# Mix to next product in a two-layer decoder trunk: tile 0 ends three weight tiles early, its first transposes move into the mix, the next product goes two chunks ahead

## Chip, cores and metric

The kernel runs on one core of a Trainium2 chip, as one launch. The metric is device time in microseconds, the median of several runs. Engines are named as in the profile: PE (TensorE matmul), PEld (its weight loads), DVE (VectorE), ACT (ScalarE), POOL (GpSimd), SP (the queue that issues the loads).

## The reference, cut to what matters

256 tokens of width 2048 pass two layers. Layer 0 mixes with a Mamba-2 block, layer 1 with sliding-window attention on one shared K/V; each layer has a SwiGLU network of width 5632. Around every sub-layer stands an RMS norm before and one after:

```
h = h + rmsnorm(mix, g[1])
ffn = (silu(u @ w_gate) * (u @ w_up)) @ w_down      # u = rmsnorm(h, g[2])
h = h + rmsnorm(ffn, g[3])
k, v = split(rmsnorm(h, kv_norm_w) @ w_kv)           # once, between the layers
```

So at four places a product ("mix") of 256 x 2048 is normed, added to h, normed again and multiplied by the next weights. Three of them have a product behind them, and those are where the change lies.

## The kernel before

Everything is float32. A float32 operand is split into a high part in the matmul's own format and a low rest, and a product is three matmuls: high by high, high by low, low by high (lines 293 to 295). Weights are streamed by `Weights`: raw tiles of 512 KB in five buffers, filled by SP; ACT casts the high part (`whi`, line 77), DVE subtracts the low part (`wlo`, line 78), into **four** converted buffers each. One converted tile ("weight tile" from here on) holds 2 x 128 rows of the contraction by 512 columns; with one token tile it makes 6 matmuls, with both 12. For K/V and q the cast carries a scale, in two halves or four quarters (lines 73 and 74). A converted buffer is free once its last matmul has read it.

The 256 tokens are two tiles t = 0, 1 of 128. `mix_stage` makes the mix in four column chunks c of 512, each chunk and tile in a PSUM bank; there are eight banks, and the mix fills them all. For the last chunk the weight tiles at the end (`lag` of them) are held: tile 0 takes all of them first, then tile 1, so that tile 0 is done while tile 1 still works. When a tile is done, ACT squares the chunk (line 351), DVE makes the mean (`ms`, line 187), POOL the power -0.5 (`rs`, line 189), and DVE multiplies the chunk by the gain (line 354).

`a_first` is the product behind a mix. For a chunk c and a tile t its `step` adds the mix to h on DVE (`add_residual`, line 398: one bank to one chunk of h), transposes that chunk of h by four PE matmuls with the identity (line 205) into a bank, and splits the four pieces into high (ACT, line 214) and low (DVE, line 215) in `xx`; for K/V, which has no gain here, the whole chunk is split at once (lines 181 and 182). `prod` then makes the matmuls of chunk c and tile t. Since the row factor is only applied to the result, the product can start before the whole row is known: `row_factor` squares the new h on ACT (line 197, eight of 128 x 512) and yields the factor (`ms` on DVE, `rs` on POOL). The gate product's result passes through Silu with that factor as scale. After K/V, `to_row` puts the two factors on a diagonal (`dg`, DVE) and multiplies it by ones on PE (line 450), for q.

Each engine runs its own queue in order. The order is made when the program is built, by a scheduler with priorities: `tc.high_priority()` moves work ahead, `tc.keep_in_program_order` holds an instruction at its written place.

Of the kernel before, what the change touches and what calls it, by code (L numbers as in the profile page):

```python
# [10 lines left out]
AF = mybir.ActivationFunctionType  # L11
# [3 lines left out]
P = 128  # L15
T = 256
NT = 2
# [80 lines left out]
def tile_yoco(ctx: ExitStack, tc: tile.TileContext, a: dict):  # L98
# [92 lines left out]

    def norm_stats(pool, h, t):
        ss = pool.tile([P, 4], F32, tag="ss", name="ss", bufs=4)
        for c in range(4):
            hs = h[:, t, CW * c : CW * (c + 1)]
            junk = pool.tile([P, CW], mybir.dt.bfloat16, tag="junk", name="junk", bufs=2)
            nc.scalar.activation(junk[:], hs, AF.Square, accum_out=ss[:, c : c + 1])  # L197
        return rstd_of(pool, ss[:], D)

    def to_xt(src, t, c, g, xt):  # L200

        xh, xl, _ = xt
        pt = bank()
        for k in range(4):
            nc.tensor.transpose(pt[:, P * k : P * (k + 1)], src[:, P * k : P * (k + 1)], ident[:])  # L205
        if g is None:
            split_bank(xh[:, 4 * c : 4 * c + 4, P * t : P * (t + 1)], xl[:, 4 * c : 4 * c + 4, P * t : P * (t + 1)],
                       pt[:].rearrange("p (k t) -> p k t", k=4))
            return
        for k in range(4):  # L210
            kt = 4 * c + k
            ps = pt[:, P * k : P * (k + 1)]
            dh = xh[:, kt, P * t : P * (t + 1)]
            nc.scalar.activation(dh, ps, AF.Copy, scale=g[:, kt : kt + 1])  # L214
            nc.vector.scalar_tensor_tensor(xl[:, kt, P * t : P * (t + 1)], ps, g[:, kt : kt + 1],  # L215
                                           dh.bitcast(F32), ALU.mult, ALU.subtract)
# [123 lines left out]

    def mix_stage(key, xt, kts, layer, which, bk0=None, hook=None, lag=2):

# [14 lines left out]
        for c in range(4):  # L357
# [15 lines left out]
            else:  # L373
# [25 lines left out]

    def a_first(key, mix, g, xt):  # L400

        xh, xl = xt[:2]
        done = [0, 0]

        def update(c, t):
            while done[t] < min(c + 1, 4):
                add_residual(mix, t, done[t])
                done[t] += 1  # L410

        def step(c, t):
            with tc.high_priority():
                update(c, t)
                to_xt(h[:, t, CW * c : CW * (c + 1)], t, c, g, xt)
                update(c + 1, t)

        bk = []

        def prod(c, t, subs):  # L420
            if len(bk) == t:
                bk.append(bank())
            for n, (hi, lo, _, per) in enumerate(subs):
                for kk in range(per):
                    a_mm(bk, xh, xl, hi, lo, kk, 4 * c + SUB * n + kk, KD, 0, CW, ts=(t,))
# [12 lines left out]
        return bk  # L438

    def row_factor():  # L440

        return [norm_stats(hpool, h, t) for t in range(NT)]

# [15 lines left out]

    def ffn(layer, mix):  # L460
        xt = new_xt()
        with tc.tile_pool(name="ffn%d" % layer, bufs=1, side="right") as fp:
# [22 lines left out]
            for u in range(FF // CW):  # L485
                if u == 0:
                    gb = a_first("gate%d_%d" % (layer, u), mix, gt[:, layer, 2, :], xt)
# [13 lines left out]
    mix = mix_stage("wout", (yh, yl), DI // P, 0, 1, bk0=bk0)  # L501
    ypool.__exit__(None, None, None)
    mix = ffn(0, mix)


    with tc.tile_pool(name="attn", bufs=1, side="right") as ap:
        xt = new_xt()
        kvb = a_first("kv", mix, None, xt)
# [3 lines left out]
        mix = mix_stage("wo", ot, KD, 1, 1, hook=hook)  # L512


    mix = ffn(1, mix)
    for t in range(NT):
# [451 lines left out]
```

## Time and profile before

| what | value |
|---|---|
| median of 3 runs | 2436.85 us (2436.16 to 2437.26) |
| the profiled execution | 2436.95 us, span 2435.2 us |
| PE busy | 2405.5 us (99%), 11760 matmuls |
| DVE busy | 1450.1 us (60%) |
| ACT busy | 1222.4 us (50%) |
| DMA | 453.75 MB, mean 186 GB/s |
| chain that ended last | PE 95%, DVE 2%, ACT 2%, DMA 1% |

The span is the profiled execution from its first to its last instruction; the rest of the time lies around it. A matmul's row gives the line, the engine, `out<-in` by the program's names, and in brackets the idle time before it with what ended it. Matmuls overlap, so the start of one to the start of the next is their pace, not their duration.

### The profile page before, as it was taken

Reading aid. Unit: us, or ns where it says so; the run is one execution under the profiler, and the core shown is the slowest. Engines: PE = TensorE matmul, PEld = TensorE weight load, DVE = VectorE, ACT = ScalarE, POOL = GpSimd, SP = SyncE. Lnnn points to the kernel's source line nnn. Section 1 sums busy time; section 2 is a strip of 40 time slices with the busy share of each in tenths; the row PEclk is TensorE's granted clock in tenths of the full one; section 3 lists DMA queues with packets and bytes.
Section 4 is the critical chain, followed back from the end, with each engine's and each line's share of the span. In section 5 each row is a group of like instructions: output and inputs, shape, how many; then the busy total and the mean of one; then the engine's idle time right before and its main releaser. Section 6 shows DMA issues by size and latency. Waiting matters only on the chain.

```text
span 2435.2 us, 30881 instructions
## 1 busy us (share of the span) xinstructions
PE 2405.5 (99%) x11760; PEld 1995.0 (82%) x11760; DVE 1450.1 (60%) x2016; ACT 1222.4 (50%) x1733; POOL 82.7 (3%) x66
## 2 busy tenths in 40 slices
PE   7999999999999999999999999999999999999998
PEld 6888888888878888888888878777888888888887
DVE  6788888875464545445444468865545445454444
ACT  6576766664454444444444457755544444444443
POOL 1500000000000000000000000000000000000000
PEclk9999999999999999999999999999999999999999
DMA  6666666657656666666666664445666666666664
GB/s 202 175 205 193 191 189 191 187 175 244 192 166 196 188 189 193 185 191 191 204 194 193 194 192 152 130 126 160 199 190 190 185 194 186 191 191 206 194 194 145
DMA packets 283892, 453.75 MB, mean 186 GB/s; under 512 B 16976, under 2 KB 115536, under 8 KB 282976
## 3 DMA queue, kind: packets, MB, share of 16 engines
q1 hardware_dynamic: 283568, 451.45, 61.8%
q8 instruction: 92, 1.51, 0.3%
q14 instruction: 56, 0.46, 0.1%
q10 hardware_dynamic: 144, 0.26, 0.0%
q0 software_dynamic: 32, 0.07, 0.0%
HBM read 449.56 MB, written 2.16 MB: 185 GB/s over the span
## 4 chain that ended last, share of the span: by engine, by line
PE 95%; DVE 2%; ACT 2%; DMA 1%; issue 1%; POOL 0%; SPq 0%; DVEq 0%; POOLq 0%; ACTq 0%
PE bank L294 23%; PE bank L295 23%; PE bank L293 23%; PE bank L235 13%; PE bank L240 7%; PE bank L479 1%; DVE wlo L78 1%; PE bank L846 1%; PE bank L889 1%; PE bank L684 1%; ACT xx L214 0%; PE bank L881 0%; ACT junk L197 0%; PE bank L205 0%; ACT whi L77 0%
## 5 line engine op out<-in xcount | busy, mean ns | idle before, releaser
L78 DVE TENSOR_TENSOR wlo<-raw,whi 128x1024 fp32r<-128x1024 f32 x785 | 960.2, 1224 | 881.0 <-ACT whi L77 880.5
L77 ACT CAST whi<-raw 128x1024 fp32r<-128x1024 f32 x785 | 826.3, 1053 | 1000.1 <-PE bank L295 910.8
L293 PE MATMUL bank<-whi,xx 128*128 128x512 f32 x1440 | 562.4, 391 | 2.5 <-ACT xx L214 2.1
L295 PE MATMUL bank<-whi,xx 128*128 128x512 f32 x1440 | 560.9, 390 | 0.9 <-DVE xx L215 0.9
L294 PE MATMUL bank<-wlo,xx 128*128 128x512 f32 x1440 | 560.8, 390 | 0.5 <-DVE wlo L78 0.5
L235 PE MATMUL bank<-xx,whi 128*128 128x512 f32 (+1 forms) x1552 | 547.1, 398 | 2.4 <-ACT whi L77 1.7
L240 PE MATMUL bank<-xx,wlo 128*128 128x256 f32 (+1 forms) x1552 | 431.7, 285 | 1.0 <-ACT xx L214 1.0
L235 PEld LDWEIGHTS bank<-xx,whi 128*128 128x128 f32 (+1 forms) x1552 | 288.5, 188 | 66.4 <-ACT whi L77 2.2
L293 PEld LDWEIGHTS bank<-whi,xx 128*128 128x128 f32 x1440 | 270.3, 188 | 60.4 <-ACT xx L214 4.2
L295 PEld LDWEIGHTS bank<-whi,xx 128*128 128x128 f32 x1440 | 270.3, 188 | 58.9 <-DVE xx L215 2.8
L294 PEld LDWEIGHTS bank<-wlo,xx 128*128 128x128 f32 x1440 | 270.4, 188 | 56.3 <-DVE wlo L78 1.4
L240 PEld LDWEIGHTS bank<-xx,wlo 128*128 128x128 f32 (+1 forms) x1552 | 292.4, 189 | 13.5 <-issue 6.6
L293 PE MATMUL bank<-whi,hh 128*128 128x512 f32 x704 | 274.0, 389 | 0.0
L295 PE MATMUL bank<-whi,hl 128*128 128x512 f32 x704 | 274.0, 389 | 0.0
L294 PE MATMUL bank<-wlo,hh 128*128 128x512 f32 x704 | 273.9, 389 | 0.0
L294 PEld LDWEIGHTS bank<-wlo,hh 128*128 128x128 f32 x704 | 132.1, 188 | 27.6
L293 PEld LDWEIGHTS bank<-whi,hh 128*128 128x128 f32 x704 | 132.1, 188 | 27.3
L295 PEld LDWEIGHTS bank<-whi,hl 128*128 128x128 f32 x704 | 132.1, 188 | 27.3
L293 PE MATMUL bank<-whi,yh 128*128 128x512 f32 x256 | 100.1, 391 | 0.0
L295 PE MATMUL bank<-whi,yl 128*128 128x512 f32 x256 | 99.7, 390 | 0.0
L294 PE MATMUL bank<-wlo,yh 128*128 128x512 f32 x256 | 99.6, 389 | 0.0
L189 POOL TENSOR_TENSOR rs<-ms,neghalf 128x1 f32<-128x1 f32 x8 | 4.4, 545 | 1816.2 <-DVE ms L187 1816.2
(164 smaller groups left out, 1714.8 us busy)
## 6 DMA issues: line engine op xcount, KB each, us to landing
raw<-in_ffn_w_gate_dram SPq DMA_DIRECT2D x176, 512.0 KB, 4.3
raw<-in_ffn_w_up_dram SPq DMA_DIRECT2D x176, 512.0 KB, 3.7
raw<-in_ffn_w_down_dram SPq DMA_DIRECT2D x176, 512.0 KB, 4.9
raw<-in_ssm_w_in_dram SPq DMA_DIRECT2D x161, 512.0 KB, 4.4
raw<-in_ssm_w_out_dram SPq DMA_DIRECT2D x64, 512.0 KB, 4.8
raw<-in_attn_w_q_dram SPq DMA_DIRECT2D x32, 512.0 KB, 3.5
raw<-in_attn_w_o_dram SPq DMA_DIRECT2D x32, 512.0 KB, 4.4
crow<-cumd SPq DMA_DIRECT2D x32, 256.0 KB, 3.9
```

Of the source, the lines that this page charges most:

```text
L77: nc.scalar.copy(hi[:], src)
L78: nc.vector.tensor_tensor(lo[:], src, hi[:].bitcast(F32), ALU.subtract)
L189: nc.gpsimd.tensor_tensor(rs[:], ms[:], neghalf[:], ALU.pow)
L235: nc.tensor.matmul(o, wh, xx[:, kt, :, :].rearrange("p a t -> p (a t)"), start=(kt == 0), stop=(kt == kts - 1))
L240: nc.tensor.matmul(o[:, :T], wl, xx[:, kt, 0, :], start=False, stop=False)
L293: nc.tensor.matmul(o, sh, wh, start=(kt == 0), stop=False)
L294: nc.tensor.matmul(o, sh, wl, start=False, stop=False)
L295: nc.tensor.matmul(o, sl, wh, start=False, stop=(kt == kts - 1))
L479: nc.tensor.transpose(pt[:, P * k : P * (k + 1)], scr[:, NT + t, P * k : P * (k + 1)], ident[:])
L684: nc.tensor.matmul(o[64 * q : 64 * q + 64, c0 : c0 + T], xdt[0][:, 2 * h2 + q, :], m[:, q, 0:T], start=True, stop=False)
L846: nc.tensor.matmul(pss[q][:, c0:c1], qt[pr, i, (0 if c0 == 0 else P) : (P if c0 == 0 else T)], kd[pr, j, 0:kn], start=True, stop=True)
L889: nc.tensor.matmul(ob[64 * q : 64 * q + 64, c0 : c0 + T], v[:, 0, vs], pt[:, q, 0:T], start=True, stop=False)
```

## The change

`lag` goes from two to three held weight tiles for the output projection, the down projection of layer 0 and the attention output; the last down projection keeps its four. `a_first` becomes a class `First`: its first `step` (residual of tile 0, four transposes, split) is issued from inside the mix, after the first of the last weight tile's two contraction rows for tile 1, and the rest in `product`, which runs two chunks of tile 0 and then the same two of tile 1, in half-chunk pieces with a `step` between them. The transposes and the squares of `row_factor` are kept in program order.

```
-    def norm_stats(pool, h, t):
+    def norm_stats(pool, h, t, pin=False):
...
-            nc.scalar.activation(junk[:], hs, AF.Square, accum_out=ss[:, c : c + 1])
+            sq = nc.scalar.activation(junk[:], hs, AF.Square, accum_out=ss[:, c : c + 1])
+            if pin:
+                tc.keep_in_program_order(sq)
...
+            tr = nc.tensor.transpose(pt[:, P * k : P * (k + 1)], src[:, P * k : P * (k + 1)], ident[:])
+            if pin:
+                tc.keep_in_program_order(tr)
...
-    def mix_stage(key, xt, kts, layer, which, bk0=None, hook=None, lag=2):
+    def mix_stage(key, xt, kts, layer, which, bk0=None, hook=None, lag=3, early=None):
...
                     for hi, lo, s, per in held:
                         for kk in range(per):
                             a_mm(bk, xh, xl, hi, lo, kk, SUB * s + kk, kts, 0, CW, ts=(t,))
+                            if early is not None and t == 1 and s == nsub - 1 and kk == 0:
+                                early((bks, rs))
...
-        step(0, 0)
-        for c in range(4):
-            subs = [W.next(key) for _ in range(4 // SUB)]
-            prod(c, 0, subs)
-            if c == 0:
-                step(0, 1)
-            if c < 3:
-                step(c + 1, 0)
-            prod(c, 1, subs)
-            if c < 3:
-                step(c + 1, 1)
-        return bk
+        def early(self, mix):
+            self.mix = mix
+            self.step(0, 0)
...
+            for c in (0, 2):
+                a, b = ([W.next(key) for _ in range(4 // SUB)] for _ in range(2))
+                prod(c, 0, a[:1])
+                self.step(c + 1, 0)
+                prod(c, 0, a, 1)
+                prod(c + 1, 0, b[:1])
+                if c == 0:
+                    self.step(0, 1)
+                prod(c + 1, 0, b, 1)
+                self.step(c + 1, 1)
+                prod(c, 1, a[:1])
+                if c == 0:
+                    self.step(2, 0)
+                prod(c, 1, a, 1)
+                prod(c + 1, 1, b[:1])
+                if c == 0:
+                    self.step(2, 1)
+                prod(c + 1, 1, b, 1)
...
-        return [norm_stats(hpool, h, t) for t in range(NT)]
+        return [norm_stats(hpool, h, t, pin=True) for t in range(NT)]
...
-            return mix_stage("down%d_" % layer, (hh, hl), KF, layer, 3, hook=hook, lag=2 if layer == 0 else CVB)
+            return mix_stage("down%d_" % layer, (hh, hl), KF, layer, 3, hook=hook, lag=CVB if early is None else 3,
+                             early=early)
```

How it moves instructions, at two places. First DVE, from the last weight tiles of the output projection into the first gate product; `wlo` is the low part of a weight tile, `h` a residual update, `xx` the low part of one transposed piece, `ms` the mean of a tile of the mix, `bank<-bank,gpost` the multiplication by the gain. Before:

```order
L78 TENSOR_TENSOR wlo<-raw,whi 128x1024 x15
L187 TENSOR_SCALAR ms<-mss,pre 128x1
L354 TENSOR_TENSOR bank<-bank,gpost 128x512
L398 SCALAR_TENSOR_TENSOR h<-bank,rs,h 128x512 x3
L215 SCALAR_TENSOR_TENSOR xx<-bank,gt,xx 128x128
L187 TENSOR_SCALAR ms<-mss,pre 128x1
L398 SCALAR_TENSOR_TENSOR h<-bank,rs,h 128x512 x2
L215 SCALAR_TENSOR_TENSOR xx<-bank,gt,xx 128x128
L398 SCALAR_TENSOR_TENSOR h<-bank,rs,h 128x512 x2
L215 SCALAR_TENSOR_TENSOR xx<-bank,gt,xx 128x128 x3
L78 TENSOR_TENSOR wlo<-raw,whi 128x1024
L215 SCALAR_TENSOR_TENSOR xx<-bank,gt,xx 128x128 x10
```

One more low part of a weight tile stood ahead of the first mean, and one in the rows after it. The same place now, in two consecutive pieces, the first up to the second update of tile 1:

```order
L78 TENSOR_TENSOR wlo<-raw,whi 128x1024 x14
L187 TENSOR_SCALAR ms<-mss,pre 128x1
L359 TENSOR_TENSOR bank<-bank,gpost 128x512
L405 SCALAR_TENSOR_TENSOR h<-bank,rs,h 128x512 x4
L219 SCALAR_TENSOR_TENSOR xx<-bank,gt,xx 128x128
L78 TENSOR_TENSOR wlo<-raw,whi 128x1024
L187 TENSOR_SCALAR ms<-mss,pre 128x1
L219 SCALAR_TENSOR_TENSOR xx<-bank,gt,xx 128x128
L405 SCALAR_TENSOR_TENSOR h<-bank,rs,h 128x512
L219 SCALAR_TENSOR_TENSOR xx<-bank,gt,xx 128x128
L405 SCALAR_TENSOR_TENSOR h<-bank,rs,h 128x512
```

All four updates of tile 0 now come in a row, and the second weight tile's low part behind them. It goes on, up to the fourth weight tile's:

```order
L219 SCALAR_TENSOR_TENSOR xx<-bank,gt,xx 128x128 x2
L405 SCALAR_TENSOR_TENSOR h<-bank,rs,h 128x512
L219 SCALAR_TENSOR_TENSOR xx<-bank,gt,xx 128x128
L78 TENSOR_TENSOR wlo<-raw,whi 128x1024
L219 SCALAR_TENSOR_TENSOR xx<-bank,gt,xx 128x128
L359 TENSOR_TENSOR bank<-bank,gpost 128x512
L219 SCALAR_TENSOR_TENSOR xx<-bank,gt,xx 128x128
L405 SCALAR_TENSOR_TENSOR h<-bank,rs,h 128x512
L78 TENSOR_TENSOR wlo<-raw,whi 128x1024
```

Three low parts of weight tiles stand among the eight updates, where one came behind seven. The third junction has the same rows.

Second ACT, at the end of the K/V product: `junk,ss<-h` is a square of the new h, `whi<-raw,gkv` a half cast of a K/V weight tile, `whi<-raw,gt 128x256` a quarter cast of one of q, `xx<-bank` the high part of a transposed chunk, `kk` the keys with their row factor. Before:

```order
L181 CAST xx<-bank 128x4x128 x2
L197 ACTIVATE junk,ss<-h 128x512 x4
L181 CAST xx<-bank 128x4x128 x4
L73 ACTIVATE whi<-raw,gkv 128x512 x4
L197 ACTIVATE junk,ss<-h 128x512
L181 CAST xx<-bank 128x4x128
L73 ACTIVATE whi<-raw,gkv 128x512 x4
L73 ACTIVATE whi<-raw,gt 128x256 x8
L824 ACTIVATE kk<-bank,rs 128x4x64 x2
```

The squares stood among the splits, the last one ahead of all of q's casts. Now:

```order
L181 CAST xx<-bank 128x4x128
L73 ACTIVATE whi<-raw,gkv 128x512 x3
L181 CAST xx<-bank 128x4x128 x2
L197 ACTIVATE junk,ss<-h 128x512 x2
L73 ACTIVATE whi<-raw,gt 128x256 x12
L197 ACTIVATE junk,ss<-h 128x512 x6
L860 ACTIVATE kk<-bank,rs 128x4x64 x4
```

Six of the eight squares now stand behind twelve casts of q. On PE the first multiplication of the diagonal (`bank<-dg,ones_pp`) stands right behind the last K/V matmul in both; the second has moved ten rows later.

More of the change, by code (lines that the diff above doesn't have):

```diff
@@ L204, in to_xt @@
         for k in range(4):
-            nc.tensor.transpose(pt[:, P * k : P * (k + 1)], src[:, P * k : P * (k + 1)], ident[:])
+            tr = nc.tensor.transpose(pt[:, P * k : P * (k + 1)], src[:, P * k : P * (k + 1)], ident[:])
+            if pin:
+                tc.keep_in_program_order(tr)
         if g is None:
@@ L398, in add_residual, with __init__, update, step @@
         nc.vector.scalar_tensor_tensor(hs, bks[c][t][:], rs[t][:, 0:1], hs, ALU.mult, ALU.add)
[L400 to L412, printed above, removed]
-            with tc.high_priority():
[L414 to L425, printed above, removed]
-        step(0, 0)
-        for c in range(4):
-            subs = [W.next(key) for _ in range(4 // SUB)]
-            prod(c, 0, subs)
-            if c == 0:
-                step(0, 1)
-            if c < 3:
-                step(c + 1, 0)
-            prod(c, 1, subs)
-            if c < 3:
-                step(c + 1, 1)
-        return bk
+    class First:
+        def __init__(self, g):
+            self.g, self.xt, self.mix, self.done = g, new_xt(), None, [0, 0]
+        def update(self, c, t):
+            while self.done[t] < min(c + 1, 4):
+                add_residual(self.mix, t, self.done[t])
+                self.done[t] += 1
+        def step(self, c, t):
+            with tc.high_priority():
+                self.update(c, t)
+                to_xt(h[:, t, CW * c : CW * (c + 1)], t, c, self.g, self.xt, pin=True)
+                self.update(c + 1, t)
+        def early(self, mix):
+            self.mix = mix
+            self.step(0, 0)
+        def product(self, key):
+            xh, xl = self.xt[:2]
+            bk = []
+            def prod(c, t, subs, first=0):
+                if len(bk) == t:
+                    bk.append(bank())
+                for n in range(first, len(subs)):
+                    hi, lo, _, per = subs[n]
+                    for kk in range(per):
+                        a_mm(bk, xh, xl, hi, lo, kk, 4 * c + SUB * n + kk, KD, 0, CW, ts=(t,))
+            for c in (0, 2):
[16 more added lines that the diff above has]
+                prod(c + 1, 1, b, 1)
+            return bk
@@ L458, in by_row, with ffn @@
                                 rr[:].unsqueeze(1).broadcast_to([P, 2, T]), ALU.mult)
-    def ffn(layer, mix):
-        xt = new_xt()
+    def ffn(layer, first, early=None):
+        xt = first.xt
         with tc.tile_pool(name="ffn%d" % layer, bufs=1, side="right") as fp:
@@ L486, in ffn @@
                 if u == 0:
-                    gb = a_first("gate%d_%d" % (layer, u), mix, gt[:, layer, 2, :], xt)
+                    gb = first.product("gate%d_%d" % (layer, u))
                     rs = row_factor()
@@ L497, in ffn, with early_kv @@
                 todo += [None, lambda u=u: store(u)]
-            return mix_stage("down%d_" % layer, (hh, hl), KF, layer, 3, hook=hook, lag=2 if layer == 0 else CVB)
-    mix = mix_stage("wout", (yh, yl), DI // P, 0, 1, bk0=bk0)
+            return mix_stage("down%d_" % layer, (hh, hl), KF, layer, 3, hook=hook, lag=CVB if early is None else 3,
+                             early=early)
+    first = First(gt[:, 0, 2, :])
+    mix_stage("wout", (yh, yl), DI // P, 0, 1, bk0=bk0, early=first.early)
     ypool.__exit__(None, None, None)
-    mix = ffn(0, mix)
+    kv = []
+    def early_kv(mix):
+        kv.append(First(None))
+        kv[0].early(mix)
+    ffn(0, first, early_kv)
     with tc.tile_pool(name="attn", bufs=1, side="right") as ap:
-        xt = new_xt()
-        kvb = a_first("kv", mix, None, xt)
+        xt = kv[0].xt
+        kvb = kv[0].product("kv")
         rs = row_factor()
@@ L511, in tile_yoco, with early_ffn @@
                              to_row(rs), by_row, fold)
-        mix = mix_stage("wo", ot, KD, 1, 1, hook=hook)
-    mix = ffn(1, mix)
+        f1 = []
+        def early_ffn(mix):
+            f1.append(First(gt[:, 1, 2, :]))
+            f1[0].early(mix)
+        mix_stage("wo", ot, KD, 1, 1, hook=hook, early=early_ffn)
+    mix = ffn(1, f1[0])
     for t in range(NT):
```

2 lines of the change are left out of this document (1 added, 1 removed).

## The prediction

> **What bounds the kernel now.** I read the page first, for its busy shares and the chain that ended last.
>
> ```profile
> span 2435.2 us, 30881 instructions
> PE 2405.5 (99%) x11760; PEld 1995.0 (82%) x11760; DVE 1450.1 (60%) x2016; ACT 1222.4 (50%) x1733; POOL 82.7 (3%) x66
> ```
>
> TensorE is busy for 99% of the span, so a microsecond is won or lost only where PE itself stands. The matmuls that the change leaves alone are the same in number and shape; what it can move is the time that PE loses at the three places where a mix ends and the next product begins (output projection to first gate, down projection to K/V, attention output to second gate). I call them J1, J2 and J3 and took their windows next, with the line of the transposes. Columns are length, then busy time and instruction count of PE, PEld, DVE, ACT, POOL.
>
> ```profile
> 695.00:736.00 41.00, 39.12 (x182) 30.66 (x181) 30.87 (x61) 28.23 (x67) 2.16 (x4) 1.00 0.51 159
> 1430.00:1461.40 31.40, 30.17 (x145) 24.02 (x145) 25.45 (x50) 23.19 (x53) 4.30 (x13) 1.00 0.58 191
> 1688.00:1730.00 42.00, 40.23 (x186) 31.50 (x185) 31.22 (x61) 30.01 (x68) 2.15 (x4) 1.00 0.52 160
> L205 PE MATMUL bank<-ident,h x96: 270/272/331, 698.4 to 1706.2; 128*128 128x128 f32 x96
> ```
>
> A busy PE is not a PE at its pace, so I also need what one matmul and one group of transposes cost when nothing holds them: the first and the last of 28 unbroken matmuls, and a group of four transposes with the matmul behind it.
>
> ```profile
> 1455.15 0.39 PE L295 MATMUL bank<-whi,xx 128*128 128x512 f32 x1
> ...
> 1461.27 0.39 PE L295 MATMUL bank<-whi,xx 128*128 128x512 f32 x1
> ...
> 712.67 0.60 PE L205 MATMUL bank<-ident,h 128*128 128x128 f32 x4
> 713.03 0.48 PE L294 MATMUL bank<-wlo,xx 128*128 128x512 f32 x1
> ```
>
> 27 steps in 6.12 us are 0.227 us a matmul; four transposes take 0.36 us, and the matmul behind them runs 0.48 instead of 0.39, so each break costs about 0.1 more. Each window has 32 of the 96 transposes (2.88 us), and two of its counted instructions began before it. J1: 148 matmuls x 0.2267 = 33.55, and 41.0 - 33.55 - 2.88 = 4.6 us lost. J2: 31.4 - 111 x 0.2267 - 2.88 = 3.3. J3: 42.0 - 152 x 0.2267 - 2.88 = 4.6. **12.5 us in all** is what a perfect version of this change could touch, less than 0.6% of the time.
>
> **What holds PE at J1.** The rows of its first microseconds, and the DVE and ACT rows that give the price of each kind of work:
>
> ```profile
> 695.57 0.39 PE L293 MATMUL bank<-whi,yh 128*128 128x512 f32 x1
> 695.77 0.60 ACT L351 ACTIVATE junk<-bank 128x512 bf16<-128x512 f32 x1 [1.67 <-PE bank L295]
> 696.49 0.21 DVE L187 TENSOR_SCALAR ms<-mss,pre 128x1 f32<-128x1 f32 x1 [1.13 <-ACT junk L351]
> 697.51 2.07 DVE L398 SCALAR_TENSOR_TENSOR h<-bank,rs,h 128x512 f32<-128x512 f32 x3 [0.20 <-POOL rs L189]
> 698.36 0.63 PE L205 MATMUL bank<-ident,h 128*128 128x128 f32 x4
> 699.03 0.37 ACT L214 ACTIVATE xx<-bank,gt 128x128 fp32r<-128x128 f32 x1 [0.84 <-PE bank L205]
> ...
> 704.08 1.22 DVE L78 TENSOR_TENSOR wlo<-raw,whi 128x1024 fp32r<-128x1024 f32 x1
> 705.21 0.61 DVE L215 SCALAR_TENSOR_TENSOR xx<-bank,gt,xx 128x128 fp32r<-128x128 f32 x2
> ...
> 707.09 1.39 DVE L215 SCALAR_TENSOR_TENSOR xx<-bank,gt,xx 128x128 fp32r<-128x128 f32 x5 [0.16 <-ACT xx L214]
> ```
>
> Tile 1's first held matmul starts at 695.57; tile 0's residual updates start 1.94 us later on DVE, after ACT's square, the factor on DVE and the power on POOL (1.02 us from ms to h). A residual update takes (2.07 - 0.74) / 2 = 0.665 us of DVE, a low part of a transposed piece (1.39 - 0.35) / 4 = 0.26, a low part of a weight tile 1.13 (704.08 to 705.21). Over the next eight microseconds DVE is full. PE waits there for DVE's queue, not for the transposes as such.
>
> **The change at J1 and J3.** With three held tiles instead of two, tile 1 has 18 matmuls (4.08 us) after tile 0 ends, so the first transposes at last stand behind ready data: h is done at 1.94 + 0.74 = 2.7 us, PE comes to them after 15 matmuls at 3.4. That is the gain. The price is in the weights. Only four converted tiles exist; three are held, so before tile 0 ends only one tile of the next product is converted, where it was two. And the new product runs two chunks of tile 0 first, which uses four different weight tiles in its first 24 matmuls, where the old one used two. In the order of DVE's queue, the low part of the fourth weight tile stands behind 8 residual updates, 8 low parts of pieces, 3 low parts of weight tiles, one factor and one multiplication by the gain (0.13 and 0.6 by their rows):
>
> 8 x 0.665 + 8 x 0.26 + 3 x 1.13 + 0.73 = 11.5 us, plus some 0.7 us in which DVE stands until POOL has tile 1's factor and for its last write. Begun at 1.94, it ends at 14.2. PE wants that tile at its 37th matmul, with three groups of transposes ahead: 37 x 0.2267 + 3 x 0.36 = 9.5 us. So PE has lost 4.7 us by then, as much as in the whole of J1 before. Bounds: if PE waits for none of the work that is not its own, 0; if every handover adds 0.1, 5.5. I take 4.7, since DVE was as full before.
>
> After that, pieces come in time: a hi part on ACT and its lo part on DVE alternate, about 0.85 us a piece by their rows, and PE needs 1.36 us for two pieces with two banks under way; I allow 0.5, and 0.1 for each of the five later groups. Last come the eight squares, now pinned behind every piece. ACT's rows at J2 and the table load of J3:
>
> ```profile
> 1436.61 0.62 ACT L197 ACTIVATE junk<-h 128x512 bf16<-128x512 f32 x1
> 1437.22 0.62 ACT L197 ACTIVATE junk<-h 128x512 bf16<-128x512 f32 x1
> ...
> 1447.15 0.64 ACT L197 ACTIVATE junk<-h 128x512 bf16<-128x512 f32 x1
> 1718.31 1.28 ACT L492 ACT_TABLE_LOAD   x1 [1.66 <-PE bank L295]
> 1719.60 0.69 ACT L492 ACTIVATE scr<-bank,rs 128x512 f32<-128x512 f32 x1
> 1720.19 1.04 ACT L77 CAST whi<-raw 128x1024 fp32r<-128x1024 f32 x1
> ```
>
> Counted from PE's last read of the buffer that the third tile of the up product takes: 0.43 to ACT, cast 0.95, one piece 0.25, eight squares 8 x 0.61 = 4.9, tile 1's factor 1.2, its Silu 0.6, then the fourth tile's cast 1.05 and its low part 1.27: 10.65 us. PE has 43 matmuls and a short wait until it needs it, 10.2. So 0.45 us are lost at J1, and 1.1 at J3, where the 1.28 us table load falls into the same queue but hides most of the factor. Together J1 4.7 + 0.5 + 0.5 + 0.5 = 6.2 and J3 6.8, against 4.6 and 4.6: **+1.6 and +2.2**.
>
> **The change at J2.** The rows for DVE's and ACT's work there, and the end of the K/V product:
>
> ```profile
> 1443.39 2.48 DVE L182 TENSOR_TENSOR xx<-bank,xx 128x512 fp32r<-128x512 f32 x4
> 1446.45 2.07 DVE L74 SCALAR_TENSOR_TENSOR wlo<-raw,gkv,whi 128x512 fp32r<-128x512 f32 x3
> 1453.02 0.21 DVE L167 TENSOR_REDUCE ms<-ss 128x1 f32<-128x4 f32 x2
> 1454.04 0.29 DVE L449 TENSOR_SCALAR dg<-ident,rs 128x128 f32<-128x128 f32 x1 [0.59 <-POOL rs L172]
> 1454.90 3.31 ACT L73 ACTIVATE whi<-raw,gt 128x256 fp32r<-128x256 f32 x8 [2.74 <-PE bank L295]
> ...
> 1461.50 0.38 PE L450 MATMUL bank<-dg,ones_pp 128*128 128x128 f32 x2
> ```
>
> The start goes as at J1: 8 x 0.665 + 3 whole chunks x 0.6 + 6 half tiles x 0.665 + 0.73 = 11.8 of DVE from 1.94, with 0.5 of standing ends at 14.2, where PE would be at 40 matmuls and three groups, 10.1. That is 4.1, and 0.6 for breaks: 4.7, against 3.3 before.
>
> The end is the large term. PE multiplies the diagonal of row factors (dg) right behind the last K/V matmul, before and after. Before, the last square was done by 1447.8, dg at 1454.3, and PE came at 1461.5: seven microseconds of cover. Now ACT has two squares, then twelve casts of q pieces, then the other six squares. Counted from the start of the last transposes: 0.67 to ACT, split 0.5, two squares 1.22, twelve casts x 0.40 = 4.8, one more square 0.61, the last to DVE 0.72, reduction to dg 1.02 (1453.02 to 1454.04), dg 0.3: 9.85 us. PE is there after 0.36 + 24 x 0.227 + 0.1 = 5.9. **PE stands for 4.0 us.** The second dg is due four squares (2.4 us) later, and PE has 2.45 us of work until it: no further wait. Lower bound 2.5, if q's casts start with no square ahead of them; upper 5.
>
> Such a stand has a second price. Three consecutive windows near the start (granted clock is the third number from the right):
>
> ```profile
> 23.21:26.62 3.41, 1.65 (x8) 0.95 (x6) 3.35 (x10) 3.01 (x9) 0.00 (x0) 1.00 0.71 133
> 26.62:30.03 3.41, 3.41 (x12) 2.90 (x12) 1.99 (x8) 1.68 (x4) 0.00 (x0) 0.50 0.48 145
> 30.03:33.45 3.42, 3.42 (x21) 2.88 (x21) 2.35 (x5) 1.82 (x6) 0.00 (x0) 1.00 0.15 25
> ```
>
> One window of 3.41 us in which PE was busy for 1.65 was followed by one at half clock, with 12 instructions where the next had 21: 3.41 x (1 - 12/21) = 1.5 us lost. A stand of 4.0 us leaves some such window busy for at most 1.4 wherever the edges fall, so I add 1.5. [...]
>
> J2 in all: 4.7 + 4.0 + 0.1 + 1.5 = 10.3 against 3.3, **+7.0**. The longer hold of the weights delays no load that counts: raw tiles are four ahead, and DMA is at 0.51 to 0.58 in these windows. Tail and start keep their order: 0.
>
> Sum: 1.6 + 2.2 + 7.0 = +10.8 us. The profiled execution took 2436.95 (span 2435.2 and 1.7 around it), 0.1 above the median: 2447.7.
>
> **Rivals.**
> - Faster: the earlier transposes hide what they are meant to, DVE finishes in PE's 9.5 us, and of 12.5 us only the 24 breaks (2.4) remain. With the dg wait of 5.6 still paid that is -10.1 + 5.6 = -4.5, 2432.4. It decides if DVE's 11.5 us shrink below 7.6; the rows above, with DVE full before, speak against it.
> - No change: J1, J2's start and J3 cost what they cost now and only the dg wait without the slow clock comes on top: 2441. The dg row speaks for it; DVE's extra weight tile against.
> [...]
> - Worse: J1 and J3 also fall under half busy in one window each, 2 x 1.5, and the squares' delay makes the up product wait twice: 2453.
>
> **How the numbers follow.** What a measurement tells from no change is 0.2%, 4.9 us. My sum 0.50; the same with the clock up 0.16; worse 0.10; no change 0.16; faster 0.08. The range reaches from 2440 to 2453. Slower by over 0.2%: 0.78; same 0.15; faster 0.07.
>
> **What would show it.** A PE wait of about 4 us on dg at the end of the K/V product, with a half-clock window behind it; PE waits on wlo at the third and fourth weight tile of each gate product, over 1 us each; eight squares in one run on ACT ahead of the Silu. If PE never waits on dg, or DVE is not full in the first 12 us of J1, I am wrong.

## The result, and the profile after

The changed kernel takes **2450.57 us** (median of 4 runs, 2448.8 to 2452.25) against 2436.77 (median of 4, 2436.16 to 2437.26): ratio 1.0055, 95% interval 1.004 to 1.007. It is slower by 13.8 us, where +10.8 was forecast. The profiled execution took 2450.87 us.

The first lines of its page:

```profile
span 2449.2 us, 30868 instructions
PE 2412.5 (99%) x11760; PEld 1997.5 (82%) x11760; DVE 1450.8 (59%) x2016; ACT 1225.5 (50%) x1733; POOL 83.9 (3%) x66
```

The same stretches of the three junctions as before (J3's moved on by 10 us, since the kernel is that much later there). Columns are length, then busy time and instruction count of PE, PEld, DVE, ACT, POOL; then granted clock, DMA share, GB/s:

```profile
695.00:736.00 41.00, 38.53 (x177) 29.16 (x175) 28.61 (x58) 28.17 (x64) 2.19 (x4) 1.00 0.44 136
1430.00:1461.40 31.40, 28.14 (x129) 21.77 (x128) 20.91 (x34) 14.41 (x25) 3.76 (x11) 0.95 0.52 166
1698.00:1740.00 42.00, 40.27 (x179) 30.80 (x178) 28.88 (x58) 28.38 (x64) 2.17 (x4) 0.96 0.46 138
```

Every engine does the same work as before, and PE's share still reads 99%. The windows tell more. J1 has 177 PE instructions in 41 us, where it had 182. J2 has 129 in 31.4 us instead of 145, at a mean clock of 0.95.

A sharper reading is possible because both kernels issue exactly 11,760 PE instructions: the n-th of one trace is set against the n-th of the other, and the growth of the distance between two such numbers is what PE lost there. From number 3780 (before J1) on, the changed kernel loses:

| stretch of PE's instructions | forecast | measured |
|---|---|---|
| J1, start and gate product (3780 to 3936) | +1.1 | +1.10 |
| J1, up product (to 3990) | +0.45 | +0.55 |
| J2, start and K/V product (7078 to 7210) | +1.4 | **+3.76** |
| J2, dg and first q product (to 7294) | +5.6 | **+5.45** |
| J3, start and gate product (8400 to 8620) | +1.1 | +1.79 |
| J3, up product (to 8700) | +1.1 | +1.15 |

The six sum to +13.8, and outside them the two traces differ by 0.3 us or less. Now the rows. First the waits of PE (in all, times, longest), the first row in the kernel before, the others now:

```profile
PE bank L294 <- DVE wlo L78: 0.5, 2, 0.3
...
PE bank L298 <- DVE wlo L78: 4.2, 5, 1.3
PE bank L472 <- DVE dg L471: 3.9, 1, 3.9
PE bank L298 <- DVE wlo L74: 2.8, 2, 2.5
```

Before, dg did not stand in this list, and all waits on weight tiles' low parts came to those 0.5 us. The timeline of ACT, DVE and PE at the end of the K/V product:

```profile
1462.58 0.62 ACT L197 ACTIVATE junk<-h 128x512 bf16<-128x512 f32 x1
...
1463.19 4.89 ACT L73 ACTIVATE whi<-raw,gt 128x256 fp32r<-128x256 f32 x12
...
1466.54 0.39 PE L299 MATMUL bank<-whi,xx 128*128 128x512 f32 x1
...
1467.99 0.61 ACT L197 ACTIVATE junk<-h 128x512 bf16<-128x512 f32 x1
...
1470.35 0.29 DVE L471 TENSOR_SCALAR dg<-ident,rs 128x128 f32<-128x128 f32 x1 [0.66 <-POOL rs L172]
...
1470.78 0.67 PE L472 MATMUL bank<-dg,ones_pp 128*128 128x128 f32 x2 [3.86 <-DVE dg L471]
```

Two squares, twelve casts of q's weights (4.89 us), then the other squares: dg comes at 1470.35, while PE has been through since 1466.9. The clock windows around this wait, around the wait of 2.5 us at J2's start, and at J3's start (PE's busy time is the first number after the length, the granted clock the third from the right):

```profile
1440.17:1443.58 3.41, 0.95 (x5) 0.68 (x5) 3.41 (x6) 0.00 (x0) 0.00 (x0) 1.00 0.18 70
1443.58:1446.99 3.41, 3.41 (x11) 2.33 (x9) 2.61 (x5) 0.59 (x1) 0.00 (x0) 0.50 0.75 219
...
1467.48:1470.89 3.41, 0.11 (x1) 0.14 (x2) 1.72 (x6) 3.41 (x11) 0.54 (x1) 1.00 0.85 256
1470.89:1474.30 3.41, 3.41 (x12) 3.02 (x13) 0.99 (x4) 3.09 (x10) 0.54 (x1) 0.50 0.41 135
...
1706.41:1709.82 3.41, 1.99 (x7) 0.86 (x6) 3.41 (x8) 1.10 (x3) 0.00 (x0) 1.00 0.36 135
1709.82:1713.23 3.41, 3.41 (x10) 2.77 (x11) 2.77 (x5) 0.52 (x2) 0.00 (x0) 0.50 0.52 154
```

Between the first 40 us and the last 6 us (where both kernels go to half clock) three windows of the changed kernel run at half clock, where the kernel before has none. One was forecast, the one behind dg.

J2's start is the place that the forecast left too cheap. The way of token tile 1's factor there (ms on DVE, the power rs on POOL, the residual update on DVE) in the timeline:

```profile
1435.96 0.43 POOL L846 IOTA dm<- 128x128 f32 x2 [3.02 <-ACT xx L181]
...
1436.84 1.04 POOL L848 TENSOR_SCALAR_AFFINE_SELECT dm<-dm 128x128 f32<-128x128 f32 x2
1436.87 0.21 DVE L187 TENSOR_SCALAR ms<-mss,pre 128x1 f32<-128x1 f32 x1
...
1438.51 0.29 POOL L848 TENSOR_SCALAR_AFFINE_SELECT dm<-dm 128x128 f32<-128x128 f32 x1
1438.77 0.54 POOL L189 TENSOR_TENSOR rs<-ms,neghalf 128x1 f32<-128x1 f32 x1
...
1439.35 1.41 DVE L405 SCALAR_TENSOR_TENSOR h<-bank,rs,h 128x512 f32<-128x512 f32 x2 [1.62 <-POOL rs L189]
...
1442.73 0.50 PE L298 MATMUL bank<-wlo,xx 128*128 128x512 f32 x1 [2.46 <-DVE wlo L74]
```

By my estimate from ms's row (it ends at 1437.08) the power could run at about 1437.2, but POOL is building the attention bias (dm, nine instructions from 1435.96), which stands ahead of it in POOL's queue: it runs at 1438.77, and DVE stands 1.62 us for it. Everything behind it on DVE is late by as much, up to the low part that PE waits 2.46 us for.

At J1 the rows are those of the forecast: PE waits for the low parts of the third and the fourth weight tile. The fourth one ended on DVE at 708.10, 14.0 us after tile 1's first held matmul, where 14.2 was forecast. At J3 PE waits for the third alone (1.32 us); the half-clock window starts there, and PE, slower in it (10 instructions in 3.41 us), finds the fourth ready. Then comes one wait in each up product (the last row of J1, and the last of all).

```profile
705.24 0.50 PE L298 MATMUL bank<-wlo,xx 128*128 128x512 f32 x1 [1.31 <-DVE wlo L78]
...
708.15 0.50 PE L298 MATMUL bank<-wlo,xx 128*128 128x512 f32 x1 [0.82 <-DVE wlo L78]
...
737.29 0.50 PE L298 MATMUL bank<-wlo,xx 128*128 128x512 f32 x1 [0.23 <-DVE wlo L78]
...
1709.74 0.74 PE L298 MATMUL bank<-wlo,xx 128*128 128x512 f32 x1 [1.32 <-DVE wlo L78]
...
1743.15 0.50 PE L298 MATMUL bank<-wlo,xx 128*128 128x512 f32 x1 [0.53 <-DVE wlo L78]
```

The first four transposes moved less than the edit suggests. In the changed kernel they stand three matmuls ahead of the mix's end on PE, at all three places; in the kernel before the scheduler had already put them one matmul ahead of it.

### The profile page after: what moved, and what is told of

The parts are those of the page before. It is cut to its first block, busy times and chain, and to the rows that moved or that the text cites. A ratio compares the mean times of both kernels' runs of the same rounds, so it can differ in the third digit from the quotient of the medians.

```text
span 2449.2 us, 30868 instructions
## 1 busy us (share of the span) xinstructions
PE 2412.5 (99%) x11760; PEld 1997.5 (82%) x11760; DVE 1450.8 (59%) x2016; ACT 1225.5 (50%) x1733; POOL 83.9 (3%) x66
## 4 chain that ended last, share of the span: by engine, by line
PE 94%; DVE 3%; ACT 1%; issue 1%; DMA 1%; POOL 0%; SPq 0%; DVEq 0%; POOLq 0%; ACTq 0%
PE bank L298 23%; PE bank L299 23%; PE bank L297 23%; PE bank L239 13%; PE bank L244 7%; DVE wlo L78 1%; PE bank L501 1%; PE bank L882 1%; PE bank L925 1%; DVE h L405 1%; PE bank L207 1%; PE bank L720 1%; PE bank L917 0%; ACT junk L197 0%; ACT whi L77 0%
```

## The experiments

My theory is the forecast's: DVE's queue sets the starts, the squares behind q's casts set dg, and a half-clock window follows a long stand. The rival is that the new orders of PE cost by themselves. All losses below, in us, are taken at the same six stretches against the kernel before, in each run's profiled execution; the medians stand against 2437.2 to 2437.4 us of the kernel before on the same chip.

| kernel | J1 start | J1 up | J2 start | J2 dg | J3 start | J3 up | median us | ratio, 95% |
|---|---|---|---|---|---|---|---|---|
| changed | 1.10 | 0.55 | 3.76 | 5.45 | 1.79 | 1.15 | 2450.57 | 1.004–1.007 |
| dg later | 1.12 | 0.54 | 2.96 | -0.01 | 1.31 | 1.16 | 2446.32 | 1.0021–1.0046 |
| bias early | 0.98 | 0.55 | 1.79 | 5.45 | 1.66 | 1.16 | 2449.41 | 1.0035–1.006 |
| one chunk | 1.97 | 2.26 | 0.44 | 7.24 | 2.23 | 4.30 | 2455.49 | 1.0059–1.0086 |
| unpinned | 1.03 | 0.00 | 2.95 | 0.11 | 1.80 | 0.00 | 2444.06 | 1.0016–1.0037 |
| before + pin | 0.34 | 0.61 | 0.16 | 6.87 | 0.29 | 1.19 | 2446.73 | 1.0022–1.005 |
| unpinned, bias early | 1.01 | 0.00 | 1.77 | 0.11 | 1.83 | 0.00 | 2441.98 | 1.001–1.0028 |
| the same, POOL low parts | -0.56 | 0.00 | 1.79 | -0.03 | 0.22 | 0.00 | 2438.46 | 0.9993–1.0012 |
| the same, lag 2 | 1.14 | 0.02 | 1.60 | -0.05 | 1.92 | 0.00 | 2441.89 | 1.0011–1.0029 |
| lag 2, POOL low parts | 0.50 | 0.01 | 1.59 | -0.03 | 1.27 | 0.00 | 2440.40 | 1.0005–1.0023 |
| the same, one chunk | 3.24 | 0.14 | -0.07 | 0.17 | 3.65 | 0.01 | 2445.41 | 1.0019–1.0044 |
| before + bias, POOL low parts | -0.71 | 0.00 | -0.94 | 0.10 | -0.43 | 0.00 | 2434.98 | 0.9981–0.9999 |

**dg later.** The diagonal's multiplication goes into the hook that holds the K transposes:

```diff
-                             to_row(rs), by_row, fold)
+                             lambda: to_row(rs), by_row, fold)
...
+    def rows():
+        rowf.append(rr())
+        k_rows()
-    queue = [lambda: None, k_rows]
+    queue = [lambda: None, rows]
```

> The changed kernel with one edit: the multiplication by the diagonal of row factors (dg) stands two weight tiles into the first q product, with the K transposes, instead of right behind the K/V product. My theory: the squares that stand behind q's casts make dg late, PE stood 3.9 us for it and ran the next window at half clock (5.4 us by the matmul count of the two traces). Now PE comes to dg some 5 us later: wait on dg under 0.5 us, no half-clock window behind it, 5.4 us less than the changed kernel, 2445.2. Rival A: the wait is not dg's own but that of the row factors, and the K transposes behind them wait as long: 2449 to 2450.6. Rival B: q's weight tiles are late as well, so that half of it comes back as waits on wlo: 2447.5 to 2448.5.

PE came to dg without a wait, and no window between the first 40 and the last 6 us ran at half clock:

```profile
1471.66 0.40 PE L239 MATMUL bank<-xx,whi 128*128 128x512 f32 x1
1471.90 0.38 PE L472 MATMUL bank<-dg,ones_pp 128*128 128x128 f32 x2
1472.12 0.60 PE L868 MATMUL bank<-ident,kk 128*128 128x128 f32 x4
```

The whole 5.45 us at this stretch went, and neither rival shows. The median fell by 4.3 only; the profiled execution, 2444.55, was the shortest of five, and it had no half-clock window at J2's and J3's start either, where the changed kernel's had one each. At J2 PE's longest wait was the same, 2.47 us against 2.46, but an edge of the windows fell inside it and left 1.79 and 2.57 us of busy time in its two windows, where the changed kernel's had 0.95 in one. So whether this wait came with a half-clock window was luck of the edges, and the price at J2 was 0.80 us. Where the other four executions had such windows was not recorded; the two longest show a mean clock of 0.996 and 0.997 against 0.998, which speaks for some.

**Bias early.** The dm tile is taken from the pool of h and built as soon as that exists; of all queues only POOL's order changes.

```diff
     h = hpool.tile([P, NT, D], F32, tag="h", name="h")
+    dm = hpool.tile([P, 384], F32, tag="dm", name="dm")
+    for c0, base in ((0, 0), (P, P), (T, 0)):
...
-    dm = ap.tile([P, 384], F32, tag="dm", name="dm")
-    for c0, base in ((0, 0), (P, P), (T, 0)):
```

> The changed kernel with one edit: the nine POOL instructions that build the attention bias (dm) are issued early, ahead of the first mix, so that at J2 the power for token tile 1 no longer stands behind them on POOL; all other queues keep their order. My theory: at J2 the power waited 1.9 us for them, DVE stood 1.6 us, and that is what my 4.7 us for J2's start left out. Without it J2's start loses 1.1 to 1.6 us less, and PE's longest wait there (2.5 us, on wlo) shrinks to about 1.2; if the window around it is then over half busy, the half-clock window goes too, 1.2 more: 2447.8 to 2449.4, most likely 2448.2. Rival: DVE is full all the same and only shuffles its order: 2450.6. At J1 and J3 nothing changes under either.

J2's start lost 1.97 us less, and its half-clock window went with it. Against the run with dg later, which has no window there either, it is 2.96 - 1.79 = 1.17 us, and that is the bias alone. The same rows as above:

```profile
1437.71 0.21 DVE L188 TENSOR_SCALAR ms<-mss,pre 128x1 f32<-128x1 f32 x1
...
1438.06 0.92 POOL L190 TENSOR_TENSOR rs<-ms,neghalf 128x1 f32<-128x1 f32 x1 [4.29 <-DVE ms L188]
...
1439.01 1.41 DVE L414 SCALAR_TENSOR_TENSOR h<-bank,rs,h 128x512 f32<-128x512 f32 x2 [0.44 <-POOL rs L190]
...
1442.39 0.50 PE L299 MATMUL bank<-wlo,xx 128*128 128x512 f32 x1 [1.29 <-DVE wlo L75]
```

POOL now waits for DVE and not the other way round; DVE stands 0.44 instead of 1.62 us, and PE 1.29 instead of 2.46. The median, 2449.41, is at the edge of what I expected.

**One chunk.** The product's order of before, with the rest of the change:

```diff
-            for c in (0, 2):
-                a, b = ([W.next(key) for _ in range(4 // SUB)] for _ in range(2))
...
+            for c in range(4):
+                subs = [W.next(key) for _ in range(4 // SUB)]
+                prod(c, 0, subs)
+                if c == 0:
+                    self.step(0, 1)
+                if c < 3:
+                    self.step(c + 1, 0)
+                prod(c, 1, subs)
+                if c < 3:
+                    self.step(c + 1, 1)
```

> The changed kernel with the product's order of before: one chunk of token tile 0, then one of tile 1, two weight tiles at a time; the three held tiles, the early transposes and the pins stay. My theory: DVE's work is what PE waits for, whatever the order. In this order the low parts of tile 1's first chunk stand behind 7 residual updates, 8 pieces, 2 low parts of weights and 0.9 of others, 9.9 us, where PE comes after 7.5 us from tile 1's start: 5 us lost by then, as with two chunks (4.7). The waits move from wlo to the transposed pieces (xx) and the update of h; J1, J2's start and J3 keep their loss within 1 us each, and dg still waits 3 to 4 us: 2449 to 2452. Rival: four weight tiles in the first 24 matmuls are the cause; with two the start costs less than before, 2 us less at each of the three: 2444.5.

Here I missed: 2455.49, above my range. The rival holds at J2's start alone, which lost 0.44 instead of 3.76; at J1 and J3 the starts got 0.9 and 0.4 worse, as the DVE theory allows. What I had left out is that the last piece comes later in this order, and the pinned squares with it: dg lost 7.24 instead of 5.45 (two half-clock windows instead of one), the up products 2.26 and 4.30. With the rest of the change, the order two chunks ahead makes the pin of the squares cheaper. The order alone does not explain the up products: in the kernel before with the pin, which also goes one chunk at a time, they lose 0.61 and 1.19.

**Unpinned.**

```diff
-        return [norm_stats(hpool, h, t, pin=True) for t in range(NT)]
+        return [norm_stats(hpool, h, t) for t in range(NT)]
```

> The changed kernel with the squares unpinned: they float ahead of and between the transposed pieces on ACT. My theory: dg's wait and the half clock behind it go (5.4 us less), and the late waits at the up products go (0.5 at J1, 1.0 at J3), but 8 squares x 0.61 us now stand among ACT's first pieces and give back 0 to 1.5 us at each of the three places: 2443.6 to 2448, most likely 2445.5. Rival A: pieces come so late that each start loses 3 us more: 2452. Rival B: the dg wait has another cause than the squares and stays at 3 to 4 us: 2450.

2444.06, in the range. dg and both up products lose nothing (0.11, 0.00, 0.00), and the starts keep their loss (1.03, 2.95, 1.80; J2's is lower by its half-clock window, which is not there). The pin of the squares costs 5.45 + 0.55 + 1.15 = 7.2 us and buys nothing at the starts, though eight squares now stand among ACT's first pieces.

**Before + pin.** The other way round, the pin alone on the kernel before:

```diff
-            nc.scalar.activation(junk[:], hs, AF.Square, accum_out=ss[:, c : c + 1])
+            sq = nc.scalar.activation(junk[:], hs, AF.Square, accum_out=ss[:, c : c + 1])
+            if pin:
+                tc.keep_in_program_order(sq)
```

> The kernel before with one part of the change alone: the squares of the row factor pinned behind the last transposed piece; its lag, its transposes and its product's order stay. My theory: the pin is what makes dg late and the up products wait. In this order the last piece comes 12 matmuls later than in the changed kernel, so the squares do too: the run with one chunk at a time lost 7.2 us at dg, 2.3 at the first up product and 4.3 at the second, and the same is due here, while the three starts lose nothing or gain up to 1 us each since ACT has no squares there: 2437 + 7.2 + 2.3 + 4.3 - 0 to 3 = 2448 to 2451. Rival: it is the earlier transposes and the chunk order that cost; the pin by itself costs the 3.9 us of dg at most, as the order of before has slack: 2437 to 2441.

The mechanism holds, the size was too high: 2446.73, of it 6.87 at dg, and 0.61 and 1.19 at the up products, where I had copied 2.3 and 4.3 from the run before. ACT and PE at dg:

```profile
1463.08 1.71 ACT L73 ACTIVATE whi<-raw,gt 128x256 fp32r<-128x256 f32 x4 [2.08 <-PE bank L297]
...
1464.69 0.61 ACT L197 ACTIVATE junk<-h 128x512 bf16<-128x512 f32 x1
...
1468.70 0.77 PE L452 MATMUL bank<-dg,ones_pp 128*128 128x128 f32 x2 [4.30 <-DVE dg L451]
```

The squares start only behind q's casts here too, and PE's wait on dg of 4.30 us brings two half-clock windows. So this pin, alone on the kernel before, makes 9.5 us, where the whole change makes 13.8.

**What is left: two edits together.**

> The changed kernel with two edits that were run apart: squares unpinned, and the attention bias built early on POOL. What is left of the change is three held tiles, the early transposes and the order two chunks ahead. My theory (the effects add): J1 loses 1.0 more than the kernel before, J2's start 1.8, J3 1.8, nothing at dg and the up products: 2437.4 + 4.6 = 2442.0. Rival: with the squares in front on ACT, POOL's early power finds ACT in the way and the bias edit brings nothing: 2444.

2441.98, and 4.7 us at the six stretches where 4.6 was forecast: the effects add. (That the median meets the forecast to 0.02 us is luck, the interval is some 2 us to either side.) Left are the three starts, 1.0, 1.8 and 1.8 us. J3's start lost no less than the changed kernel's, though it had no half-clock window; whether the squares, which now stand among its pieces, take the place of that window's price was not measured.

**POOL low parts.** In the converting loop, on that kernel:

```diff
+                n = len(self.cv) - self.first[key]
+                eng = nc.gpsimd if key in ("gate0_0", "gate1_0") and n in (1, 3) else nc.vector
-                nc.vector.tensor_tensor(lo[:], src, hi[:].bitcast(F32), ALU.subtract)
+                eng.tensor_tensor(lo[:], src, hi[:].bitcast(F32), ALU.subtract)
```

> The changed kernel with three edits: squares unpinned, the attention bias built early on POOL (both as in the earlier runs), and, new, the low parts of the second and the fourth weight tile of each first gate product made by POOL instead of DVE. Without the new one the sum is 2444.1 - 2.0 = 2442. My theory: DVE's queue is what PE waits for at J1 and J3; it loses 2 x 1.13 us of work there, and POOL, idle, needs about 2.6 us a tile (its 128x512 row is 1.31). J1 and J3 each lose 1.5 to 2.3 us less: 2437.4 to 2439, most likely 2438. J2's start keeps its DVE work. Rival A: POOL is so much slower that PE waits for its low parts as long as before: 2442 to 2443. Rival B: POOL's reads slow DVE's, and both starts get worse: 2444 and more.

With two low parts off DVE's queue, J1's start lost 1.57 us less and J3's 1.61, J2's (where no low part moved) the same; 2438.46 was within what the theory gave. That is the direct sign that DVE's queue is what PE waits for there. POOL and DVE at J1:

```profile
696.59 2.41 POOL L81 TENSOR_TENSOR wlo<-raw,whi 128x1024 fp32r<-128x1024 f32 x1 [0.93 <-ACT whi L78]
...
698.61 1.47 DVE L81 TENSOR_TENSOR wlo<-raw,whi 128x1024 fp32r<-128x1024 f32 x1
...
700.82 2.36 POOL L81 TENSOR_TENSOR wlo<-raw,whi 128x1024 fp32r<-128x1024 f32 x1
```

**Lag.** Two held tiles instead of three, without and with POOL's help:

```diff
-    def mix_stage(key, xt, kts, layer, which, bk0=None, hook=None, lag=3, early=None):
+    def mix_stage(key, xt, kts, layer, which, bk0=None, hook=None, lag=2, early=None):
```

> The same with two held tiles instead of three. My theory: with three held, one tile less of the next product is converted in time, and that low part (1.13 us at J1 and J3, 1.33 at J2) stands in DVE's queue at the start; with two it is out of it, while the first transposes have 1.36 us less cover (h is done at 2.7 us of tile 1, PE comes at 2.0). Net 0.5 to 1.1 us less at each of the three: 2438.7 to 2440.5, most likely 2439.7. Rival A: the order two chunks ahead is what costs, whatever the lag: 2442. Rival B: the lost cover costs more than the low part: 2443.5.

> The same with two held tiles and the low parts of the second and fourth weight tile of each first gate product on POOL. The run with three held tiles and POOL took 2438.5. My theory: J2 gets 0.5 to 1.3 us less as without POOL; at J1 and J3 the second tile is converted early anyway, so 0 to 0.5 less each: 2436.0 to 2438, most likely 2437. Rival: DVE no longer bounds J1 and J3 with POOL's help, and the lost cover of the first transposes shows in full, 0.7 more at each: 2439.

Both theories missed. The lag changes nothing (2441.89 against 2441.98), which is what rival A of the first run forecast for the case that the product's order costs. At J1 PE's waits on the low parts fall from 1.2 to 0.4 us, but those on high parts of pieces rise from 0.9 to 1.5. With POOL's help the lag of three is the better one by 1.9 us, in the direction of the second run's rival: with two held tiles PE waits up to 0.8 us for a high part of a piece at J1, with three no wait on a high part there is over 0.3.

**The versions on the kernel before.**

> The kernel before with two edits: the attention bias built early on POOL, and the low parts of the second and the fourth weight tile of each first gate product on POOL. My theory: DVE bounds the junctions of the kernel before too (it was full for the 8 us behind the first residual update), so J1 and J3 lose 1 to 2 us less each, and J2 about 0.8 less, where DVE stood 1.1 us for the power: 2432.5 to 2434.5, most likely 2433.5. Rival: PE waits there for pieces that stand ahead of these low parts in DVE's queue; then only J2's 0.8 comes: 2436.4.

2434.98, 0.5 us above the range that I gave, but **the only kernel faster than both**: ratio 0.999, interval 0.9981 to 0.9999, some 2.4 us. It takes nothing of the change. J2's 0.94 is the bias, as forecast. At J1 and J3 the low parts on POOL brought 0.71 and 0.43 us, less than the 1 to 2 of my theory: DVE is only a part of what bounds these two places in the kernel before. PE's waits on its low parts there (0.3 and 0.2) are gone, but those on the high parts that ACT makes (1.0 at each) stay, as the rival had it.

> The kernel before with the bias and POOL edits (2435.0) and one part of the change, the first transposes inside the last weight tile; two held tiles, one chunk at a time, squares unpinned. My theory: in the run without this part PE stood 0.5 and 1.0 us around the first transposes of J1 and J3, between the held matmuls and the new product, for their copies on ACT; with the transposes three matmuls earlier some 0.5 us of that is covered at each place: 2433.8 to 2434.6. Rival: the transposes stand before matmuls that could run, and wait for h there: 2435 to 2436.

A clear miss: 2445.41, with 3.2 and 3.7 us at J1 and J3. PE waited ten times on a copied piece there:

```profile
PE bank L300 <- ACT xx L221: 4.4, 10, 0.8
```

The part that I meant to test did not move. PE at the end of J1's mix, first in the kernel before, then in this one:

```profile
698.36 0.63 PE L205 MATMUL bank<-ident,h 128*128 128x128 f32 x4
698.74 0.47 PE L295 MATMUL bank<-whi,yl 128*128 128x512 f32 x1
699.45 0.50 PE L293 MATMUL bank<-whi,xx 128*128 128x512 f32 x1 [0.23 <-ACT xx L214]
...
697.38 0.63 PE L210 MATMUL bank<-ident,h 128*128 128x128 f32 x4
697.76 0.47 PE L302 MATMUL bank<-whi,yl 128*128 128x512 f32 x1
698.46 0.50 PE L300 MATMUL bank<-whi,xx 128*128 128x512 f32 x1 [0.23 <-ACT xx L221]
```

In both, four transposes, the last matmul of the mix, then the new product; the run before this one (2434.98) has the same PE order up to instruction 3804. What sets the two apart is the pin of the transposes, which this kernel kept and which holds the later groups at their written places: at J1 12 matmuls, eight transposes, 24 matmuls, eight, where the unpinned ones drift to 5, eight, 5, eight, 10, eight. So the difference between the two runs, 3.95 us at J1, 0.87 at J2's start and 4.08 at J3, lies with these later groups, as far as PE's order tells; a run with the pin of the transposes as its only edit was not made. Against the run with lag 2 and POOL low parts, this kernel differs in the product's order alone: two chunks ahead is better by 2.7 and 2.4 us at J1 and J3, and worse by 1.7 at J2's start.

**The clock by itself.** Twenty made stands of PE in the kernel before:

```diff
+            def stall(gb, n):
+                s = hpool.tile([P, P], F32, tag="stall", name="stall", bufs=1)
+                nc.vector.tensor_copy(s[:], gb[NT - 1][:, :P])
+                for _ in range(n):
+                    nc.gpsimd.tensor_tensor(s[:], s[:], ones_pp[:], ALU.mult)
+                tc.keep_in_program_order(nc.tensor.transpose(bank()[:, :P], s[:], ident[:]))
```

> The kernel before with a made stand of PE between the gate and the up product of 20 feed-forward chunks: DVE copies part of the gate's bank, POOL multiplies the copy by ones 0, 1, 2, 2, 3, 3, 4, 5, 6 and 8 times, and PE transposes it into a bank that nobody reads, ahead of the up product. Stands of about 1 to 7 us, at phases against the clock's windows that fall as they fall. Theory A: a window in which PE is busy for less than about 1.9 of its 3.41 us is followed by one at half clock, which costs 1 to 1.5 us: from stands of about 1.5 us up some, from 3.0 us up all show it; 10 to 14 half-clock windows in the 20 stands, about 2437 + 65 + 15 = 2515 us. Theory B: only a window without any PE work does it: no stand under 3.4 us, and of those between 3.4 and 6.8 us a part; 1 to 3 half-clock windows, about 2505 us.

Counted from 0.23 us (a matmul's pace) after the start of the matmul before, the stands came out at 1.27, 1.87, 3.44, 3.98, 4.51, 5.04, 5.57 and 6.63 us, 79 us in all, and 24 half-clock windows lie at them, so the time (one run, 2553.06) is above both forecasts, and theory B is out; of theory A the limit of 1.9 us is not confirmed. Of the four stands under 1.9 us none was followed by a half-clock window; of the sixteen from 3.44 us up, fifteen were. Only four of the sixteen had a window without any PE work. Two stands of the same 3.44 us at different phases:

```profile
914.47:917.88 3.41, 1.59 (x8) 0.97 (x6) 1.64 (x3) 2.30 (x3) 0.48 (x2) 1.00 0.65 196
917.88:921.29 3.41, 1.95 (x9) 1.62 (x10) 1.10 (x1) 0.00 (x0) 1.41 (x1) 1.00 0.53 160
921.29:924.71 3.42, 3.42 (x17) 2.82 (x16) 1.13 (x1) 1.05 (x1) 0.00 (x0) 1.00 0.24 93
...
1914.57:1917.98 3.41, 1.28 (x6) 0.74 (x4) 1.64 (x3) 2.30 (x3) 0.79 (x2) 1.00 0.74 229
1917.98:1921.40 3.42, 2.26 (x6) 1.88 (x7) 0.79 (x1) 0.00 (x0) 1.10 (x1) 0.50 0.53 158
1921.40:1924.81 3.41, 3.41 (x9) 2.64 (x9) 0.00 (x0) 0.04 (x1) 0.00 (x0) 0.50 0.14 54
```

The first stand falls across an edge and leaves 1.59 and 1.95 us of busy PE in its two windows: the clock stays. The second leaves 1.28 in one: the next is at half clock. From the transpose on, 61 instructions took 13.8 us without a half-clock window, 15.1 to 15.4 with one (1.3 to 1.6 us dearer) and 15.7 to 16.4 with two.

## Why the prediction was right, and where it was off

The direction, the order of the terms and nearly every place were right; 2450.57 lies in the range of 2440 to 2453. The sum was 3.0 us short, 2.4 of it at J2's start and 0.7 at J3's.

- **J1 +1.6**: measured 1.10 + 0.55 = 1.65. The waits at the third and fourth weight tile were 1.31 and 0.82, where I had said over 1 each. That DVE's queue is the cause is shown by the POOL run, where 2 x 1.22 us less of DVE work brought 1.57. The late wait at the up product belongs to the pinned squares: without the pin it is 0.00.
- **J3 +2.2**: measured 2.94. The up product's 1.15 is as forecast (1.1); the start's 1.79 has a half-clock window in it that I had priced only in the rival "worse". In the run with dg later, where no such window came, the start lost 1.31, so the window's share is about 0.5. The wait that I had put at the fourth weight tile is not there.
- **J2's start, 4.7 against 3.3**: the step that failed. I allowed 0.5 us for DVE standing, and DVE stood 1.62 for a power behind the bias on POOL; I had the DVE queue in hand and not the place of the power in POOL's. Bias early gave back 1.97 of the 3.76: 1.17 for the bias, and 0.80 for the half-clock window, which came by luck of the windows' edges. That is two thirds of the missing 3.0.
- **The dg wait, 4.0**: 3.86 in the trace. Moving dg and taking the pin away each removed it wholly, and the pin alone put 4.30 us there in the kernel before, so the squares behind q's casts are shown as the cause.
- **Half clock, +1.5**: dg's stretch lost 5.45, where wait and clock were forecast at 5.6. That the window need not be empty is shown by the made stands (1.28 us busy in the one at 1914.57) and by J2's window with 0.95 us. My bound was too loose all the same: I went by a window with 1.65 us of busy time, and with 1.59 and 1.95 us the clock stayed.
- **The rivals**: "worse" was partly true (a half-clock window at J3, none at J1); "faster" and "no change" were not; "the same with the clock up", put at 0.16, is shown by no run: the wait on dg had one half-clock window behind it in the changed kernel (1470.89 to 1474.30, clock 0.50), and two with one chunk and with the pin alone.

What makes the last 1.0, 1.8 and 1.8 us of the starts, when squares and bias are put right, is narrowed down and not closed. The third held tile is not it: with two the starts lose 1.14, 1.60 and 1.92. Nor are the first transposes, which stand on PE in that kernel where they stood before the change. What is left is the pin of the later transposes and the order two chunks ahead. In the order of one chunk at a time the pinned transposes go with 3.95, 0.87 and 4.08 us; the order two chunks ahead wins part of it back at J1 and J3 and adds to it at J2 (1.59 against -0.07 in the two runs that differ in it alone). That order with unpinned transposes was not run.

## What to carry to other kernels

Putting work "behind everything" on a queue had its price here at whoever waited for its result (3.86 us of PE on dg): follow the last consumer (here dg, seven microseconds covered before, none after) and look what else the scheduler fills in ahead. For a value that crosses three engines, look up its place in each queue; POOL's, 3% busy, held DVE back by 1.62 us. And where PE was fed by a DVE that was full for ten microseconds (9.55 us busy from 696 to 706 in the changed kernel), moving two instructions to POOL brought 1.6 us at each of two places; in the kernel before, where less hung on DVE, it was 0.7 and 0.4.

## What the runs showed of the hardware

- In all fourteen traces, between the first 40 and the last 15 us, I counted the PE work of each 3.41 us window as matmuls x 0.2265 us (a transpose 0.09; narrow matmuls are counted too high by this). All 33 windows under 1.39 us were followed by half clock. Of 136 windows with 1.40 to 2.5 us, two were, and above that one (2.8 us, at 159.78 in the kernel before with the pin); all three hold narrow matmuls, and counted by their widths they come to about 1.2, 1.2 and 1.43 us. So in these traces the two groups part near 1.4 us of counted work in a window, and this count does not make it sharper. In the changed kernel seven matmuls began in J1's window from 702.89 to 706.31 (2.06 us busy), and the next kept the full clock; six began in J3's from 1706.41, the last 0.08 us before its edge, and the next ran at half. The profile's busy time reads higher where matmuls stand alone: the window at J3 shows 1.99 us busy, and its work is about 1.2.
- POOL made a low part of 128x1024 in 2.38 us (mean of 4) where DVE takes 1.22. DVE's low part that began at 698.61, while POOL's ran until 699.00, took 1.47 instead of 1.22. That is one row, 0.25 us longer, and no run here measured what made it so.
